# A hybrid decoder layer on one core: compression's layer, the third norm and one 512-column matmul change places, and the end's scaling, joint and stores are divided anew

## The chip, the cores and the metric

The kernel runs on one core of a Trainium2 chip. The metric is the device time of one execution in microseconds; the number given for a kernel is the median of several executions. A separate execution was taken by the hardware profiler; its rows tell when each instruction ran. The engines are TensorE (PE in the profile, with its weight loads as PEld), VectorE (DVE), ScalarE (ACT), GpSimd (POOL) and SyncE (SP, which here only issues transfers). Each engine runs its own instructions in the order of its queue, and the engines wait for one another by semaphores.

## The reference

One decoder layer on 256 tokens of 1024 channels, all in float32, then a final norm:

```python
def reference(x, mem, ...):
    h = rms_norm(x, norm_mix_g)
    x = x + hybrid_mixer(h, ...)              # convolution branch and sparse attention, gated, one projection
    h = rms_norm(x, norm_x_g)
    x = x + cross_attention(h, mem, xq_w, xkv_w, xo_w)
    h = rms_norm(x, norm_ffn_g)
    x = x + swiglu(h, ffn_in_w, ffn_out_w)    # (silu(a) * b) @ w_out
    return rms_norm(x, final_norm_g)

def rms_norm(x, g):
    return x * lax.rsqrt(jnp.mean(x * x, axis=-1, keepdims=True) + EPS) * g

def compress_blocks(blocks, pos, w1, w2):     # keys and values of the attention, by blocks of 32 tokens
    z = jnp.einsum("bnlgd,lde->bnge", blocks + pos, w1)
    return jax.nn.silu(z) @ w2                # "compression's layer" below is this second product
```

## The kernel before

Activations lie with channels on the 128 partitions and tokens along the row. A weight of the projections comes in chunks of 256 columns (`u0`..`u7`, `kc`, `vc`, `q0`.., `ga0`..`ga3`, `gc0`.., `f0`..`f21` and so on), each in two halves of 512 KB that SyncE loads in the order of the list into four rotating buffers.

To keep float32's accuracy on the faster one-pass matmul, each half is split: ScalarE copies it to a rounded high part (line 184, names ending in `h`), and VectorE or GpSimd subtracts that from the original to get the low part (line 186, names ending in `l`). One chunk is then 48 matmuls of 256 columns (line 266): high by high, high by low and low by high, 16 each. `gemm` runs a chunk, `sweep` one half of it, and `rows` is the generator below both. Small products (`c_ps`, `gt_ps`, `rn`, the transposes) are done with plain float32 operands in several passes.

A chunk's result goes to a bank of PSUM, the accumulator memory: `bank()` hands out four in turn, in the stages that matter here.

The order of the work on each engine is made when the program is built: a scheduler goes through the code in the order in which it is written and places the instructions by its own model of their times. Three tools bend it. `in_line()` puts a TensorE instruction behind the last one so marked, `behind(...)` does it for any marks, and `turn(...)` chains the instructions of VectorE and of ScalarE at the very end. On the chip the order is then fixed, engine by engine.

The five places that the change and the prediction touch:

- **u chunks** (lines 494 to 502): eight chunks for the convolution branch. Ahead of `u2` stands a *settle*: one matmul of 512 columns (line 248) whose result is overwritten and not used.
- **Compression** (lines 561 to 600): `hidden()` runs the first product behind `q1`, and `compressed()` the second (`c_ps`), called from within `ga0`, behind a part of its second half. `part` then splits its result by a ScalarE copy and a VectorE subtraction into `kcp` and `vcs`. Between `vw` and `ga0` stands `g_ps`, the heads' gates, which ScalarE copies to `sgn`; `gt_ps` turns them and `sgt` is their exponential. `gt_ps` and the attention's `s0` use one and the same bank. `compressed_scores` (`cs_ps`) needs `kcp`. GpSimd makes `vcm` from `vcs`.
- **Third norm** (lines 1248 to 1266): the feed-forward stage starts on channels that aren't normalised yet. `rooted_all` sums the squares of a token over partitions (`rn`, line 359), ScalarE takes the root (line 362, with a table load ahead of it, since the engine holds one set of functions at a time), and VectorE the reciprocal (line 363). Each chunk's result is scaled by it when VectorE reads it out (`ab`, line 1264), which frees the bank. `f0` and `f1` run ahead of the norm's matmul. A settle stands ahead of `f3`.
- **The f stage's transfers**: SyncE issues the loads of `f` in order, with the eight transfers of the turned residual (line 1132) between `f4`'s first half and its second.
- **The end** (lines 1404 to 1448): the output of the layer is summed for the first 128 tokens (tb = 0) and the last 128 (tb = 1). For each, `total` adds the residual, `gained` multiplies by the final norm's gain, `square` sums squares on ScalarE, `joint` adds a part's sum to the rest, `rooted` takes the root, and `sent` inverts it, scales 672 columns on VectorE and 352 on ScalarE and stores both pieces.

Of the kernel before, what the change touches and what calls it, by code (L numbers as in the profile page):

```python
# [12 lines left out]
ALU = mybir.AluOpType  # L13
# [84 lines left out]
def tile_hybrid_block(  # L98
# [42 lines left out]
    def small(name, shape, dt=F32, tag=None, bufs=1):  # L141
        if len(shape) == 2 and shape[1] < LINE:
            return sb.tile([P, LINE], dt, tag=tag or name, name=name, bufs=bufs)[:, 0:shape[1]]
        return sb.tile(shape, dt, tag=tag or name, name=name, bufs=bufs)
# [79 lines left out]
    def halved(name, i):  # L224
        return split(raw(name, i), [P, 4, 256], f"{name}_{i}")
# [20 lines left out]
    def settle(ps, x):  # L246

        return nc.tensor.matmul(ps.rearrange("p b q -> p (b q)"), lhsT=x[:, 0, 0:P], rhs=x[:, 0:2].rearrange("p k q -> p (k q)"), start=True, stop=True)

    def settled(ps, x):  # L250

        with in_line():
            last[:] = [settle(ps, x)]
# [17 lines left out]
    def sweep(*args, **kw):  # L271
        for _ in rows(*args, **kw):
            pass
# [3 lines left out]
    def gemm(name, x, nat=False, ps=None):  # L277

        ps = bank(f"ps_{name}") if ps is None else ps
        for i in range(2):  # L280
            sweep(ps, ahead_of_x.pop(f"{name}_{i}", None) or halved(name, i), x, i, nat, name in in_order)
        return ps
# [210 lines left out]

    for j in range(NB):
        ps = bank(f"ps_u{j}")
        if j == 2:
            settle(ps, hh)
        gemm(f"u{j}", h, ps=ps)
        sg = small(f"sg{j}", [P, S], tag="sg", bufs=3)
        act = nc.scalar.activation(sg, ps[:, 1], AF.Sigmoid)  # L500
        vec = nc.vector.tensor_tensor(out=vt[j][:, PAD:], in0=ps[:, 0], in1=sg, op=ALU.mult)
        convolve(13 * (j > 0), (0, 1, 1, 1, 1, 0, 1, 1)[j], act, vec)
# [83 lines left out]
    def compressed():  # L586

        c_ps = aux("c_ps", [P, 3, HD], "o", 1)
        kc_ps, vc_ps = c_ps[:, 0].rearrange("p (g n) -> p g n", g=GROUPS), c_ps[:, 1:3]
        with in_line():  # L590
            nc.tensor.matmul(kc_ps, lhsT=ppt[:, PP_W2K:PP_W2K + P], rhs=zz[:, 0, :64].rearrange("p (g n) -> p g n", g=GROUPS),
                             start=True, stop=True)
            for i in range(2):
                mm = nc.tensor.matmul(vc_ps[:, i], lhsT=zz[:, 1, i * P:i * P + P], rhs=ppt[:, PP_W2V:PP_W2V + HD],
                                      start=True, stop=True)
        last[:] = [mm]
        part(kcp[:, :, 0], kcp[:, :, 1], kc_ps)
        part(vcs[:, 0], vcs[:, 1], vc_ps)
# [52 lines left out]
    with in_line():  # L651
        for n, x in enumerate(h):
            for kb in range(NB):
                mm = nc.tensor.matmul(g_ps, lhsT=wgs[:, kb].rearrange("p c n -> p (c n)"), rhs=x[:, kb],
                                      start=n + kb == 0, stop=n * kb == NB - 1)
    last[:] = [mm]
    sgn = small("sgn", [P, S], tag="sg", bufs=3)
    igd = small("igd", [P, HEADS, 2, 2])
    igc = small("igc", [P, 2, HEADS])
# [48 lines left out]
    def gate(j):  # L708

        ps = bank(f"ps_ga{j}")  # L710
        for i in range(2):
            for n, _ in enumerate(rows(ps, halved(f"ga{j}", i), h, i)):
                if j == 1 and i + n == 0:
                    compressed_scores(0)
                if j == 0 and (i, n) == (1, 0):
                    compressed()
        halved_tangent(j, ps)

    gate(0)
# [526 lines left out]
    nc.sync.dma_start(gf[:, 0:2], gfo)  # L1246
    homes.append(gf[:, 2:4])
    ahead_of_norm = []
    for j in range(2):
        ahead_of_norm.append(bank(f"ps_f{j}"))  # L1250
        for i in range(2):
            sweep(ahead_of_norm[j], halved(f"f{j}", i), (fg[:, 0], fg[:, 1]), i, line=j == i == 1)
    with in_line():
        rf = rooted_all([acc2], "3", ("vw", 4))
    for j in range(NF):
        if j < 2:
            ps = ahead_of_norm[j]
        else:
            ps = bank(f"ps_f{j}")
            if j == 3:  # L1260
                settle(ps, fg[:, 0])
            gemm(f"f{j}", (fg[:, 0], fg[:, 1]), ps=ps)
        ab = small(f"ab{j}", [P, 2, S], tag="pr", bufs=4)
        scaled[:] = [nc.vector.tensor_tensor(out=ab, in0=ps, in1=rf.unsqueeze(1).to_broadcast([P, 2, S]), op=ALU.mult)]  # L1264
        sl = small(f"sl{j}", [P, S], tag="sg", bufs=3)
        silu = nc.scalar.activation(sl, ab[:, 0], AF.Silu)  # L1266
        nc.vector.tensor_tensor(out=sl, in0=sl, in1=ab[:, 1], op=ALU.mult)
        marks = part(uh[j // 8][:, j % 8], ul[j // 8][:, j % 8], sl[:])
        if 8 <= j and not (j % 2 and j // 2 in SEVEN):
            with behind(*marks):  # L1270
                next(in_pieces, None)
        if j == 12:
            coming.append(paired(SEVEN[1], homes[:1]))
            coming.append(paired(SEVEN[2], [small(f"t{n}_{SEVEN[2]}", [P, 1, 512], tag="p0", bufs=2) for n in range(2)]))
        if j == 16:
            spare.append(long("spare", 10, (P, 4, 512)))
            homes.append(spare[0][:, 2:4])
            coming.append(paired(SEVEN[3], homes[1:]))
        if j // 2 in SEVEN:
            even_odd.append(sl)  # L1280
            if j % 2:
                factors(j // 2, *even_odd)
                even_odd.clear()
        if j == 2:
            turn_residual()
# [113 lines left out]
    def turn(eng, make, *args):  # L1399

        with behind(*chained.get(eng, ())):
            chained[eng] = make(*args),
# [2 lines left out]
        return nc.vector.tensor_tensor(out=ys[1][tb][:, cs], in0=ps, in1=more[2 * tb + 1][:, cs], op=ALU.add)  # L1405

    def joint(tb, n):
        return nc.vector.scalar_tensor_tensor(out=ss[:, tb, 0:1], in0=ss[:, tb, n:n + 1], scalar=1.0 / D, in1=ss[:, tb, 0:1],
                                              op0=ALU.mult, op1=ALU.add)

    def rooted(tb, n):
        return nc.scalar.activation(rr[:, tb:tb + 1], ss[:, tb, n:n + 1], AF.Sqrt, scale=1.0 / D, bias=ss[:, tb, 0:1])

    def sent(tb, eng):

        x, r, cut, rows = x3[:, tb].rearrange("p c n -> p (c n)"), rr[:, tb:tb + 1], 352, slice(tb * P, tb * P + P)
        turn("v", nc.vector.reciprocal, r, r)
        turn("v", lambda: nc.vector.tensor_scalar(out=x[:, cut:], in0=x[:, cut:], scalar1=r, scalar2=None, op0=ALU.mult))
        turn("a", lambda: nc.scalar.activation(x[:, :cut], x[:, :cut], AF.Copy, scale=r))
        eng.dma_start(out[rows, :cut], x[:, :cut])  # L1420
        nc.sync.dma_start(out[rows, cut:], x[:, cut:])

    ws = {i: half(wfo[i, :, 2:4], f"fo{i}_1") for i in range(early, NF // 2)}
    for i, w in ws.items():
# [11 lines left out]
    turn("a", square, 0, 1, wide, 1)  # L1436
    turn("a", rooted, 0, 1)
    turn("v", total, 1, steps[0], ends[0])
    turn("a", square, 1, 1, steps[0], 1)
    sent(0, nc.sync)  # L1440
    turn("v", gained, 1, 1, steps[0])
    turn("v", total, 1, steps[1], ends[1])
    turn("v", joint, 1, 1)
    turn("v", lambda: nc.vector.tensor_tensor_reduce(out=junk[:, 1, 1, steps[1]], in0=ys[1][1][:, steps[1]], in1=ys[1][1][:, steps[1]],
                                                     scale=1.0, scalar=0.0, op0=ALU.mult, op1=ALU.add, accum_out=ss[:, 1, 2:3]))
    turn("v", gained, 1, 1, steps[1])
    turn("a", rooted, 1, 2)
    sent(1, nc.scalar)


_OUTS = [((S, D), "float32")]
# [120 lines left out]
```

## Time and profile before

| | us |
|---|---|
| median of 3 executions | 527.72 |
| lowest and highest | 526.9 and 527.84 |
| the profiled execution | 526.18 |
| its span, first to last instruction | 524.4 |
| TensorE busy in it | 516.8 |
| mean granted clock of TensorE | 0.996 of full |

The views read are the page's busy shares, the waits (who waited for whom, total, times, longest), the chain of waits in order of time (start, duration, engine, what, line and number of instructions), the timeline of an engine (start, duration, engine, line, operation, output and input, shape and count; in brackets idle time before it and what ended it), and the windows. In the chain and the timeline, neighbours of one kind are merged into one row, so the duration is that of the whole row. The chain counts a matmul from the end of the one before it, the timeline from its own start, so the two differ by a fraction of a microsecond at each row.

### The profile page before, as it was taken

How to read it: one execution, taken by the hardware profiler on the slowest of the kernel's cores; microseconds unless marked ns; L12 is line 12 of the kernel's file. 1: busy time of each engine (PE TensorE's matmuls, PEld its weight loads, DVE VectorE, ACT ScalarE, POOL GpSimd, SP SyncE). 2: the span in 40 equal slices, each digit the busy share in tenths (PEclk: the TensorE clock that was granted, in tenths of full speed). 3: DMA queues.
4: the chain of work that ended last, by engine and by line, in shares of the span. 5: the costliest groups of instructions: out<-in, count | busy, mean ns of one | idle time of the engine just before them, and what ended most of it. 6: DMA issues, size and time to landing. Idle time of an engine off the chain costs nothing.

```text
span 524.4 us, 11134 instructions
## 1 busy us (share of the span) xinstructions
PE 516.8 (99%) x4287; PEld 499.9 (95%) x4287; DVE 436.2 (83%) x883; ACT 345.0 (66%) x605; POOL 160.8 (31%) x114
## 2 busy tenths in 40 slices
PE   9999999999999999999999999999999999999994
PEld 8999999999999999999999999999999999988884
DVE  4866999899979798974968586797998888779985
ACT  5585576788756988879547754756665665558553
POOL 0069999999970300300004100150000000000021
PEclk9999999999999999999999999999999999999998
DMA  8927965665435543348665663879765657755552
GB/s 317 416 94 247 362 204 162 201 206 178 161 116 173 179 163 129 128 136 227 208 203 201 234 163 119 288 223 284 258 228 197 203 179 235 221 134 187 201 125 95
DMA packets 34772, 104.69 MB, mean 200 GB/s; under 512 B 3744, under 2 KB 9376, under 8 KB 34336
## 3 DMA queue, kind: packets, MB, share of 16 engines
q1 hardware_dynamic: 32704, 99.36, 56.2%
q0 software_dynamic: 1296, 3.41, 4.0%
q10 hardware_dynamic: 720, 1.23, 0.6%
q8 instruction: 33, 0.54, 0.4%
q14 instruction: 19, 0.16, 0.1%
HBM read 100.64 MB, written 2.29 MB: 196 GB/s over the span
## 4 chain that ended last, share of the span: by engine, by line
PE 98%; DVE 1%; ACT 0%; issue 0%; DVEq 0%; ACTq 0%
PE ps_f L266 23%; PE ps_u L266 8%; PE fo L1298 6%; PE ps_v L266 4%; PE ps_ga L266 4%; PE ps_pw L266 4%; PE ps_q L266 4%; PE ps_gc L266 4%; PE ps_xo L266 4%; PE ps_xq L266 4%; PE ps_wo L266 4%; PE m L1298 4%; PE ps_k L266 3%; PE s L778 2%; PE pt_a L823 1%; PE o L844 1%
## 5 line engine op out<-in xcount | busy, mean ns | idle before, releaser
L462 DVE SCALAR_TENSOR_TENSOR yp<-vt,ppt,yp 128x256 f32<-128x256 f32 x204 | 81.6, 480 | 0.2
L266 PE MATMUL ps_f<-g,f_1h 128*128 128x256 f32 x352 | 44.4, 276 | 0.0
L266 PE MATMUL ps_f<-g,f_0h 128*128 128x256 f32 x352 | 44.0, 277 | 0.0
L266 PEld LDWEIGHTS ps_f<-g,f_1h 128*128 128x128 f32 x352 | 42.0, 188 | 0.0
L266 PEld LDWEIGHTS ps_f<-g,f_0h 128*128 128x128 f32 x352 | 41.9, 188 | 0.1
L186 DVE TENSOR_TENSOR f_1l<-f,f_1h 128x1024 fp32r<-128x1024 f32 x22 | 27.4, 1248 | 7.4 <-ACT f_1h L184 6.7
L184 ACT ACTIVATE f_1h<-f 128x1024 fp32r<-128x1024 f32 x22 | 23.3, 1059 | 15.0 <-PE ps_f L266 8.3
L184 ACT ACTIVATE f_0h<-f 128x1024 fp32r<-128x1024 f32 x22 | 23.2, 1056 | 12.4 <-issue 6.5
L186 DVE TENSOR_TENSOR f_0l<-f,f_0h 128x1024 fp32r<-128x1024 f32 x22 | 27.2, 1238 | 0.5 <-ACT f_0h L184 0.5
L186 POOL TENSOR_TENSOR u_0l<-u,u_0h 128x1024 fp32r<-128x1024 f32 x7 | 17.4, 2481 | 30.3 <-DVE kt L551 30.3
L1172 POOL DMA_DIRECT2D spare<-in_wfo_dram x1 | 0.9, 866 | 81.7 <-DVE ul L313 81.7
L266 PE MATMUL ps_f<-g,f_0l 128*128 128x256 f32 x176 | 23.7, 276 | 0.0
L266 PE MATMUL ps_f<-g,f_1l 128*128 128x256 f32 x176 | 23.6, 276 | 0.0
L266 PEld LDWEIGHTS ps_f<-g,f_0l 128*128 128x128 f32 x176 | 21.7, 188 | 0.0
L266 PEld LDWEIGHTS ps_f<-g,f_1l 128*128 128x128 f32 x176 | 21.6, 188 | 0.0
L798 ACT ACTIVATE p<-p,mins 128x256 f32<-128x256 f32 x32 | 15.9, 502 | 7.9 <-DVE mins L783 7.9
L1264 DVE TENSOR_TENSOR ab<-ps_f,r 128x512 f32<-128x512 f32 x22 | 14.9, 687 | 4.0 <-PE ps_f L266 4.0
L186 POOL TENSOR_TENSOR u_1l<-u,u_1h 128x1024 fp32r<-128x1024 f32 x7 | 18.0, 2569 | 0.0
L1266 ACT ACTIVATE sl<-ab 128x256 f32<-128x256 f32 x22 | 9.0, 418 | 12.4 <-DVE ab L1264 12.4
L474 POOL TENSOR_TENSOR yt<-yt,vw 128x512 f32<-128x512 f32 x13 | 17.1, 1319 | 0.0
L266 PE MATMUL ps_u<-hh,u_0h 128*128 128x256 f32 x128 | 16.3, 277 | 0.0
L266 PE MATMUL ps_u<-hh,u_1h 128*128 128x256 f32 x128 | 16.0, 276 | 0.0
(624 smaller groups left out, 1620.3 us busy)
## 6 DMA issues: line engine op xcount, KB each, us to landing
f<-in_wst_dram SPq DMA_DIRECT2D x44, 512.0 KB, 3.8
fo<-in_wfo_dram SPq DMA_DIRECT2D x16, 512.0 KB, 4.8
u<-in_wst_dram SPq DMA_DIRECT2D x14, 512.0 KB, 7.8
q<-in_wst_dram SPq DMA_DIRECT2D x8, 512.0 KB, 4.5
ga<-in_wst_dram SPq DMA_DIRECT2D x8, 512.0 KB, 3.7
gc<-in_wst_dram SPq DMA_DIRECT2D x8, 512.0 KB, 4.2
v<-in_wst_dram SPq DMA_DIRECT2D x8, 512.0 KB, 6.1
pw<-in_wst_dram SPq DMA_DIRECT2D x8, 512.0 KB, 4.6
```

The costliest lines, as they stand in the source:

```text
L184: copy = nc.scalar.activation(hi, w, AF.Copy)
L186: splits[name] = copy, eng.tensor_tensor(out=lo, in0=w, in1=f(hi[:]), op=ALU.subtract)
L266: mm = nc.tensor.matmul(ps[:, b], lhsT=lhsT, rhs=rhs, start=row + b + kb == 0, stop=kb == NB - 1 and row == 2 and b == 1)
L462: nc.vector.scalar_tensor_tensor(out=out[:, i] if t == ts[-1] else acc[i], in0=v, scalar=w, in1=acc[i], op0=ALU.mult, op1=ALU.add)
L474: nc.gpsimd.tensor_tensor(out=yt[:, 0:2], in0=yt[:, 0:2], in1=pr, op=ALU.add)
L778: nc.tensor.matmul(s1, lhsT=qh(hd, 1), rhs=t[:, g].rearrange("p b t -> p (b t)"), start=i == 0, stop=i == 1)
L798: exp.append(nc.scalar.activation(p1[k][:, br], p1[k][:, br], AF.Exp, scale=-1.0, bias=mins[:, hd, 1, br:br + 1], accum_out=sums[:, hd, 1, ...
L823: mm = nc.tensor.transpose(ps[:, i], src, ident)
L844: mm = nc.tensor.matmul(o_ps[HD * k:HD * k + HD, i], lhsT=vst[:, 0, br, gs], rhs=ta[k][:, 2 * br:2 * br + 2].rearrange("p t q -> p (t q)") ...
L1264: scaled[:] = [nc.vector.tensor_tensor(out=ab, in0=ps, in1=rf.unsqueeze(1).to_broadcast([P, 2, S]), op=ALU.mult)]
L1266: silu = nc.scalar.activation(sl, ab[:, 0], AF.Silu)
L1298: mm = nc.tensor.matmul(o, lhsT=a[x], rhs=b[w], start=start and n == 0, stop=stop and n == 2)
```

## The change

Five edits, none of which changes what is computed.

1. The settle ahead of `u2` is put ahead of `u1`, and `u0`'s first half is put in line with it.
2. `compressed()` is called right behind `g_ps`, and not within `ga0`.
3. `f2`'s first half runs ahead of the third norm's matmul, as `f0` and `f1` do.
4. `joint`, which adds one column to another with a factor, moves from VectorE to ScalarE, and is called earlier.
5. The first tokens' last scaling is 256 columns on VectorE and 768 on ScalarE, and was 672 and 352. They are stored in two pieces, both from SyncE's queue, the 256 columns first. The last tokens' scaling stays as it was.

```diff
     for j in range(NB):
         ps = bank(f"ps_u{j}")
-        if j == 2:
-            settle(ps, hh)
-        gemm(f"u{j}", h, ps=ps)
+        if j == 1:
+            settled(ps, hh)
+        for i in range(2):
+            sweep(ps, halved(f"u{j}", i), h, i, line=i + j == 0)
...
     last[:] = [mm]
+    compressed()
     sgn = small("sgn", [P, S], tag="sg", bufs=3)
...
                 if j == 1 and i + n == 0:
                     compressed_scores(0)
-                if j == 0 and (i, n) == (1, 0):
-                    compressed()
...
-    for j in range(2):
+    for j in range(3):
         ahead_of_norm.append(bank(f"ps_f{j}"))
-        for i in range(2):
-            sweep(ahead_of_norm[j], halved(f"f{j}", i), (fg[:, 0], fg[:, 1]), i, line=j == i == 1)
+        for i in range(2 - j // 2):
+            sweep(ahead_of_norm[j], halved(f"f{j}", i), (fg[:, 0], fg[:, 1]), i, line=j == 2)
     with in_line():
         rf = rooted_all([acc2], "3", ("vw", 4))
     for j in range(NF):
-        if j < 2:
+        if j < 3:
             ps = ahead_of_norm[j]
+            if j == 2:
+                sweep(ps, halved("f2", 1), (fg[:, 0], fg[:, 1]), 1, line=False)
...
     def joint(tb, n):
-        return nc.vector.scalar_tensor_tensor(out=ss[:, tb, 0:1], in0=ss[:, tb, n:n + 1], scalar=1.0 / D, in1=ss[:, tb, 0:1],
-                                              op0=ALU.mult, op1=ALU.add)
+        return nc.scalar.activation(ss[:, tb, 0:1], ss[:, tb, n:n + 1], AF.Identity, scale=1.0 / D, bias=ss[:, tb, 0:1])
...
-    def sent(tb, eng):
-
-        x, r, cut, rows = x3[:, tb].rearrange("p c n -> p (c n)"), rr[:, tb:tb + 1], 352, slice(tb * P, tb * P + P)
-        turn("v", nc.vector.reciprocal, r, r)
-        turn("v", lambda: nc.vector.tensor_scalar(out=x[:, cut:], in0=x[:, cut:], scalar1=r, scalar2=None, op0=ALU.mult))
-        turn("a", lambda: nc.scalar.activation(x[:, :cut], x[:, :cut], AF.Copy, scale=r))
-        eng.dma_start(out[rows, :cut], x[:, :cut])
-        nc.sync.dma_start(out[rows, cut:], x[:, cut:])
+    def inverted(tb):
+        turn("v", nc.vector.reciprocal, rr[:, tb:tb + 1], rr[:, tb:tb + 1])
+
+    def scaled_by(tb, cs, eng):
+
+        x, r = x3[:, tb].rearrange("p c n -> p (c n)")[:, cs], rr[:, tb:tb + 1]
+        if eng == "v":
+            turn("v", lambda: nc.vector.tensor_scalar(out=x, in0=x, scalar1=r, scalar2=None, op0=ALU.mult))
+        else:
+            turn("a", lambda: nc.scalar.activation(x, x, AF.Copy, scale=r))
+        return out[tb * P:tb * P + P, cs], x
...
     turn("v", total, 1, steps[0], ends[0])
+    inverted(0)
+    nc.sync.dma_start(*scaled_by(0, slice(768, 1024), "v"))
     turn("a", square, 1, 1, steps[0], 1)
-    sent(0, nc.sync)
     turn("v", gained, 1, 1, steps[0])
+    turn("a", joint, 1, 1)
+    nc.sync.dma_start(*scaled_by(0, slice(0, 768), "a"))
     turn("v", total, 1, steps[1], ends[1])
-    turn("v", joint, 1, 1)
...
     turn("a", rooted, 1, 2)
-    sent(1, nc.scalar)
+    inverted(1)
+    nc.sync.dma_start(*scaled_by(1, slice(352, 1024), "v"))
+    nc.scalar.dma_start(*scaled_by(1, slice(0, 352), "a"))
```

What stands in TensorE's queue around `ga0` and `ga1`, before (each row a line of the kernel, operation, output and inputs, shape and count):

```order
L654 MATMUL g_ps_1876<-hh_84,wgs_1873 128x256 x16
L266 MATMUL ps_ga0_1900<-hh_84,ga0_0h_1903 128x256 x16
L266 MATMUL ps_ga0_1900<-hh_84,ga0_0l_1904 128x256 x8
L266 MATMUL ps_ga0_1900<-hh_84,ga0_1h_1933 128x256 x8
L591 MATMUL c_ps_1945<-zz_351,ppt_66 128x64
L594 MATMUL c_ps_1945<-ppt_66,zz_351 128x64 x2
L266 MATMUL ps_ga0_1900<-hh_84,ga0_1h_1933 128x256 x8
L266 MATMUL ps_ga0_1900<-hh_84,ga0_1l_1934 128x256 x8
L266 MATMUL ps_ga1_1977<-hh_84,ga1_0h_1980 128x256 x8
L755 MATMUL gt_ps_2062<-cpt_67,sgn_1893 128x48 x2
L740 MATMUL cs_ps0_1992<-kcp_1172,qt_1176 128x32 x16
```

And now, from the same `g_ps` on, without three rows of `ga1`:

```order
L655 MATMUL g_ps_1876<-hh_84,wgs_1873 128x256 x16
L592 MATMUL c_ps_1893<-zz_351,ppt_66 128x64
L595 MATMUL c_ps_1893<-ppt_66,zz_351 128x64 x2
L266 MATMUL ps_ga0_1908<-hh_84,ga0_0h_1911 128x256 x16
...
L740 MATMUL cs_ps0_1992<-kcp_1172,qt_1176 128x32 x16
...
L266 MATMUL ps_ga1_1977<-hh_84,ga1_1l_2030 128x256 x8
L755 MATMUL gt_ps_2062<-cpt_67,sgn_1901 128x48 x2
L778 MATMUL s1_0_2075<-kdh_1537,qt_1176 128x512
L778 MATMUL s1_0_2075<-kdl_1538,qt_1176 128x512
L778 MATMUL s1_1_2083<-kdh_1537,qt_1176 128x512
L778 MATMUL s1_1_2083<-kdl_1538,qt_1176 128x512
L780 MATMUL s0_0_2073<-kdh_1537,qt_1176 128x256
```

Compression's three products moved 32 matmuls forward, and `gt_ps` moved back to just ahead of the first scores.

In ScalarE's queue at the third norm, before (`f4_1h` is the high part of `f4`'s second half, `r_3` the norm's root, `sl0` the first chunk's silu):

```order
L184 ACTIVATE f3_1h_4975<-f3_1_4973 128x1024
L184 ACTIVATE f4_0h_5020<-f4_0_5018 128x1024
L362 ACT_TABLE_LOAD
L362 ACTIVATE r_3_4843<-rn_3_4841,eps_t_69 128x256
L184 ACTIVATE f4_1h_5050<-f4_1_5048 128x1024
L184 ACTIVATE f5_0h_5088<-f5_0_5086 128x1024
L1266 ACT_TABLE_LOAD
L1266 ACTIVATE sl0_4848<-ab0_4846 128x256
```

And now:

```order
L184 ACTIVATE f3_1h_4975<-f3_1_4973 128x1024
L184 ACTIVATE f4_0h_5020<-f4_0_5018 128x1024
L184 ACTIVATE f4_1h_5050<-f4_1_5048 128x1024
L362 ACT_TABLE_LOAD
L362 ACTIVATE r_3_4874<-rn_3_4872,eps_t_69 128x256
L184 ACTIVATE f5_0h_5088<-f5_0_5086 128x1024
L1268 ACT_TABLE_LOAD
L1268 ACTIVATE sl0_4879<-ab0_4877 128x256
```

The high part of `f4`'s second half has moved ahead of the root and its table load.

## Prediction

> **What bounds the kernel now.** I read the page's busy shares first, then the waits, then the chain in order of time, and the timelines of single engines last. The busy shares put TensorE at 99%, with every other engine behind it:
>
> ```profile
> PE 516.8 (99%) x4287; PEld 499.9 (95%) x4287; DVE 436.2 (83%) x883; ACT 345.0 (66%) x605; POOL 160.8 (31%) x114
> ```
>
> Of waits, TensorE has one row, at the kernel's start:
>
> ```profile
> PE warm L377 <- DVE eps_t L167: 1.1, 1, 1.1
> ```
>
> So TensorE bounds all but the last microseconds. An edit ahead of the end counts only if it changes how long TensorE's own instructions take, or makes it wait. The chain (start, duration, name, instructions) shows that equal instructions do not always take equal time:
>
> ```profile
> 30.15 9.87 PE ps_u L266 x86
> ...
> 131.99 1.88 PE g_ps L654 x16
> 133.87 3.77 PE ps_ga L266 x32
> ...
> 138.26 2.79 PE ps_ga L266 x24
> 141.05 0.38 PE gt_ps L755 x4
> 141.42 1.76 PE cs_ps L740 x16
> ...
> 353.08 0.43 PE rn L359 x2
> 353.51 4.83 PE ps_f L266 x41
> 358.34 0.23 PE ps_f L248
> 358.57 103.36 PE ps_f L266 x912
> ```
>
> A 256-column matmul takes 113.3 ns in the last row (103.36/912), but 117.8 ns in the 32 ahead of compression's layer (3.77/32) and in the 41 behind the third norm (4.83/41). I call the two states quick and slow; they differ by 4.5 ns a matmul. The slow state holds until something resets it: compression's matmuls do (the 24 behind them, with one restart in the sum, average 2.79/24 = 116.3, and that restart explains most of the rest), and the 512-column matmul of L248 does. The windows (busy, instructions, granted clock) show that the clock is the same in both:
>
> ```profile
> 133.87:137.64 3.77, 3.77 (x35) 1.00 0.47 176
> 358.70:369.50 10.80, 10.80 (x97) 1.00 0.99 319
> ```
>
> **The change part by part.** The profiled execution took 526.18 us, of which its span is 524.4 and 1.78 lies around it; it is 1.54 below the median of the runs, 527.72. I make the sum against 526.18 and carry the difference over to the median. A measurement of this kernel can tell about 0.2% from no change, which is 1.06 us.
>
> *The 512-column matmul* moves from u2 to u1 and takes its 0.23 us in either place. The 86 matmuls ahead of its old place average 114.8 ns (9.87/86), one restart included, so they are quick and it resets nothing there: 0. Bounds: −0.17, were the other 38 of u1's 48 matmuls slow in other executions (38 × 4.5 ns), and +0.1 for one more restart.
>
> *Compression's layer* moves from within ga0 to right behind g_ps. The 32 matmuls of ga0 at 117.8 ns then stand behind the reset: 32 × 4.5 ns = −0.14. Its inputs are made long before, so it waits for nothing. Its two ScalarE copies now precede sgn, and gt_ps, which needs sgn, falls behind ga1, ahead of the 512-column s instead of cs_ps. The timeline of TensorE has the price of s behind such a matmul in plain float32, and then of the same s without:
>
> ```profile
> 225.23 0.50 PE L778 MATMUL s<-kdh,qt 128*128 128x512 f32 x1
> ...
> 226.03 0.39 PE L778 MATMUL s<-kdh,qt 128*128 128x512 f32 x1
> ```
>
> That is +0.11, a restart. cs_ps loses its own neighbour, which I put at −0.09, so +0.02 together. The move makes one new wait possible: s0 writes the bank of gt_ps and needs the ScalarE exponential that reads it (L758), which is queued behind sga (L706). ScalarE's rows and the first s on TensorE:
>
> ```profile
> 141.46 0.25 ACT L758 ACTIVATE sgt<-gt_ps 128x96 f32<-128x96 f32 x1 [0.43 <-PE gt_ps L755]
> ...
> 147.66 0.39 PE L778 MATMUL s<-kdh,qt 128*128 128x512 f32 x1
> ...
> 147.97 0.58 ACT L706 ACTIVATE sga<-ps_ga 128x512 f32<-128x512 f32 x1
> ```
>
> Ahead of sga, gt_ps's 0.38 and the 0.14 are gone, so it starts near 147.45 and the exponential ends near 148.3. TensorE runs gt_ps until about 147.5 and then four 512-column matmuls (0.23 each), so s0 stands at 148.5. The cover is some 0.2 us; were it gone, TensorE and all behind it would wait as long. On GpSimd, vcm (4.05 us) passes ahead of ga2's last low part:
>
> ```profile
> 141.04 2.35 POOL L186 TENSOR_TENSOR ga_1l<-ga,ga_1h 128x1024 fp32r<-128x1024 f32 x1
> ...
> 146.98 4.05 POOL L725 TENSOR_TENSOR vcm<-vcs,cpt 128x512 fp32r<-128x512 f32 x4
> ```
>
> That part was done at 143.4 and is done before 149 now; ga2 begins some 3 us behind the first s and uses it 40 matmuls (4.5 us) later, near 155. The sync queue's gc loads that wait for its buffer slip by the same 5 us, within the same cover. Part: −0.14 + 0.02 = −0.12, bounds −0.25 (no restart) and +0.3 (s0 waits).
>
> *The third norm* moves behind f2's first half. Of the 41 slow matmuls 17 then stand ahead of it: 17 × 4.5 ns = −0.08. But on ScalarE, which runs its queue in order, the root now stands behind the split of f4's second half, and that split waits for its load. The rows of the sync queue, ScalarE, VectorE and TensorE:
>
> ```profile
> 352.79 1.05 SPq L221 DMA_DIRECT2D f<-in_wst_dram  x2
> ...
> 353.56 1.28 ACT L362 ACT_TABLE_LOAD   x1
> 354.85 0.48 ACT L362 ACTIVATE r<-rn,eps_t 128x256 f32<-128x256 f32 x1
> 358.80 1.06 ACT L184 ACTIVATE f_1h<-f 128x1024 fp32r<-128x1024 f32 x1 [3.47 <-DMA f<-in_wst_dram]
> ...
> 355.36 1.75 DVE L363 RECIPROCAL r<-r 128x256 f32<-128x256 f32 x1 [0.56 <-ACT r L362]
> 359.89 1.23 DVE L186 TENSOR_TENSOR f_1l<-f,f_1h 128x1024 fp32r<-128x1024 f32 x1 [2.78 <-ACT f_1h L184]
> 361.03 1.88 DVE L1264 TENSOR_TENSOR ab<-ps_f,r 128x512 f32<-128x512 f32 x3
> ...
> 363.85 1.98 PE L266 MATMUL ps_f<-g,f_0h 128*128 128x256 f32 x16
> ```
>
> Before, the root was done at 355.33, and ScalarE's 3.47 us wait for the load delayed nothing else. Now the root waits it out too: split 358.80 to 359.86, table load to 361.14, root to 361.63, reciprocal to 363.41 (VectorE has done f4's low part by then), the first ab (1.88/3) to 364.1. Four banks hold f0 to f3, so f4 starts when that ab has freed f0's. TensorE gets there at 363.85 − 0.12 − 0.08 = 363.65: it waits 0.45, and restarts for 0.11 as above. f5's bank is freed 0.6 later and needed 5.4 later, so this is the only wait; VectorE's rows behind it have that much room as well. The landing decides its size: half a microsecond earlier and nothing is left of it, one later and it is 1.6. Part: −0.08 + 0.56 = +0.48, bounds −0.08 and +1.5.
>
> The Trainium skill ("ScalarE: Activation LUTs", section "What ACT_TABLE_LOAD costs") puts a switch of tables at about 2.66 us, the load and a drain of 1.38 together. By that the root would come 1.38 us later and the sum would be as much higher, 529.3 against the median. The rows speak against it: the root starts 1.29 us behind the load's start, and I give it no chance apart from the late cases below.
>
> *The end.* VectorE and ScalarE in turn, behind TensorE's last matmul; the first row is a scaling of 256 columns elsewhere:
>
> ```profile
> 159.78 0.34 DVE L810 TENSOR_SCALAR p<-p,sums 128x256 f32<-128x256 f32 x1
> ...
> 517.33 0.57 DVE L1418 TENSOR_SCALAR x<-x,rr 128x672 f32<-128x672 f32 x1
> 517.55 0.28 PE L1298 MATMUL end<-fo_1l,uh 128*128 128x256 f32 x1
> 517.60 0.57 ACT L1419 ACTIVATE x<-x,rr 128x352 f32<-128x352 f32 x1
> 518.15 0.42 DVE L1405 TENSOR_TENSOR y<-end,more 128x256 f32<-128x256 f32 x1
> 518.60 0.43 DVE L1444 CUSTOM_DVE_ANT_0 x<-y 128x256 f32<-128x256 f32 x1
> 519.07 0.30 ACT L1412 ACTIVATE rr<-ss 128x1 f32<-128x1 f32 x1 [0.90 <-DVE ss L1444]
> ```
>
> VectorE's first scaling shrinks from 672 to 256 columns, from 0.57 to 0.34. The last sum moves from 518.15 to 517.92, still behind TensorE's end at 517.83. The joint leaves VectorE too, but the custom square began only 0.03 behind the sum's end (518.57), so its going wins 0 to 0.03. The second root could then start at 518.84 instead of 519.07. ScalarE must be free by then: at 517.60 it now does the joint (bounded by the one-column root's 0.30), then 768 columns, which cost 0.87 on the line through 352 columns (0.57) and 1024 (1.06, above). Overlapped as they are, that ends between 518.7 and 518.85: just in time. The sync queue issues three stores instead of two of these and one: 256 columns near 517.7, 768 near 518.85, 672 near 520.0, none behind another. I take −0.20, bounds −0.26 and +0.2.
>
> Sum: 0 − 0.12 + 0.48 − 0.20 = +0.16, so 526.34 for an execution like the profiled one and **527.9** against the median: no change that can be told.
>
> **The rivals.**
>
> *Slower: the wait at f4 leaves TensorE slow.* The f loop has one reset, at f3, ahead of the wait. Should TensorE restart slow, f4 to f21, 18 × 48 = 864 matmuls, cost 4.5 ns more each, 3.9 us: 531.8 against the median. For it speak the 41 behind the norm, and 40 elsewhere at 117.8 ns until transposes came:
>
> ```profile
> 230.92 4.71 PE ps_v L266 x40
> ```
>
> Against it: behind a plain wait ahead of u0 TensorE got quick by itself, 130 ns each with the restart in the first ten, then 113.8:
>
> ```profile
> 27.95 1.30 PE ps_u L266 x10
> 29.25 0.91 PE ps_k L266 x8
> ```
>
> It decides from any wait at f4, however short. Chance 0.17.
>
> *No wait: f4's load lands half a microsecond or more earlier.* The f loads land 3.8 us behind their issue in the median, this one nearer 6, so there is room for it:
>
> ```profile
> f<-in_wst_dram SPq DMA_DIRECT2D x44, 512.0 KB, 3.8
> ```
>
> Then the sum is −0.12 − 0.08 − 0.20 = −0.40: 527.3. Ordinary executions are 1.5 us longer than the profiled one, and should a part of that be slow stretches that the new places reset, the lower bounds come on top, down to 526.9. Chance 0.25, half of it near the bound or, with the runs' own scatter (their lowest is 0.8 under the median), past it.
>
> *ScalarE late at the end.* If joint and 768 columns take 0.4 us longer than I took, the second root starts 0.2 later than before instead of 0.2 earlier: 528.3. No row shows 768 columns on ScalarE. The Trainium skill ("ScalarE: Activation LUTs", section "Rules for kernel authors") gives such multiplies and adds to VectorE, which speaks for this rival. Chance 0.08.
>
> *The moves win nothing:* the states hang on something else than the order, and only the wait and the end are left, 0.22 above the forecast (with the u1 edit at 0): 528.1. The Trainium skill ("TensorE: Matmul & The Clock Gate", section "Step-by-step: what each phase is for") has weight loads run ahead, beside the running matmul, without taking from it; by that rule a 256-column matmul costs the same in every place. The 117.8 and 113.3 ns at one clock speak against it. Chance 0.05.
>
> **How the numbers follow.** The forecast has 0.45, the four rivals 0.55. Faster by over 0.2%: half of the second rival, 0.12. Slower by over 0.2%: the first, 0.17, and 0.05 of the forecast's cases, those with the load a microsecond late: 0.22. Within: 0.66. The range reaches down to 526.6 (the second rival's 526.9 and some scatter) and up to 529.4 (the forecast with the wait at its upper bound, +1.0, and a late end, +0.4); beyond it lies the first rival and little else.
>
> **What would show it.** In the profile after: ga0's 48 matmuls at about 113.5 ns; gt_ps behind ga1 and no wait at s0; the third norm's root near 361 instead of 354.85, and a wait of TensorE of about half a microsecond ahead of f4, with 113.3 ns behind it; the second root at the end about 1.3 us behind TensorE's last start instead of 1.5. Wrong would be: no wait at f4 because the load landed early, 117.8 ns through the f loop, or the second root released by ScalarE's own scaling instead of VectorE's square.

## The result, and the profile after

| | before | after |
|---|---|---|
| median of the compared executions (6 each) | 527.65 us | 531.8 us |
| lowest and highest | 526.71 and 528.33 | 530.95 and 532.58 |
| the profiled execution, its span | 526.18, 524.4 | 531.16, 529.4 |
| TensorE busy in it | 516.8 | 521.5 |
| mean granted clock | 0.996 | 0.996 |

The ratio is 1.0082, with a 95% interval of 1.0070 to 1.0094: the change makes the kernel 4.2 us slower, where no change was forecast. It is the rival with the wait at f4 that came out, at the time that it named (531.8). Of after, the busy shares of the page first:

```profile
PE 521.5 (99%) x4287; PEld 504.1 (95%) x4287; DVE 436.0 (82%) x882; ACT 344.9 (65%) x606; POOL 161.2 (30%) x114
```

TensorE has as many instructions as before and the same mean clock, and is busy 4.7 us longer. Idle time is not the cause; the instructions themselves take longer. The waits of TensorE in after have one new row of only 0.2 us:

```profile
PE warm L377 <- DVE eps_t L167: 1.1, 1, 1.1
PE ps_f L266 <- DVE ab L1266: 0.2, 1, 0.2
```

The chain of after shows what released f4, and what came behind it:

```profile
353.21 5.91 DMA f<-in_wst_dram
...
359.23 1.07 ACT f_1h L184
...
361.60 0.48 ACT r L362
...
362.11 1.76 DVE r L363
...
363.96 0.70 DVE ab L1266
364.67 0.14 issue
364.81 102.00 PE ps_f L266 x864
466.80 3.23 PE fo L1300 x14
```

The steps are those of the forecast: load, split, root, reciprocal, first read-out, f4. But the 864 matmuls of f4 to f21 take 102.00/864 = 118.1 ns each, where before the row of 912 had 113.3. That is 864 x 4.7 ns = 4.1 us by this view, and 3.91 by the starts (f4 to the first fo: 101.83 after, 97.92 before). The windows of the same stretch (its length, then busy time and instructions of PE, PEld, DVE, ACT and POOL, and the granted clock third from the end) have the clock at 1.00 in both kernels; of after:

```profile
364.81:466.60 101.79, 101.79 (x864) 101.79 (x865) 87.46 (x144) 61.62 (x94) 0.86 (x1) 1.00 0.63 203
```

So the new wait is small (0.38 us by the starts, worked out below), and the state in which it leaves TensorE costs ten times as much.

### The profile page after: what moved, and what is told of

The parts are those of the page before. It is cut to its first block, busy times and chain, and to the rows that moved or that the text cites. A ratio compares the mean times of both kernels' runs of the same rounds, so it can differ in the third digit from the quotient of the medians.

```text
span 529.4 us, 11134 instructions
## 1 busy us (share of the span) xinstructions
PE 521.5 (99%) x4287; PEld 504.1 (95%) x4287; DVE 436.0 (82%) x882; ACT 344.9 (65%) x606; POOL 161.2 (30%) x114
## 4 chain that ended last, share of the span: by engine, by line
PE 95%; DMA 2%; DVE 1%; ACT 1%; issue 0%; ACTq 0%; DVEq 0%; SPq 0%
PE ps_f L266 20%; PE ps_u L266 8%; PE fo L1300 6%; PE ps_v L266 4%; PE ps_ga L266 4%; PE ps_pw L266 4%; PE ps_q L266 4%; PE ps_gc L266 4%; PE ps_xo L266 4%; PE ps_xq L266 4%; PE ps_wo L266 4%; PE m L1300 4%; PE ps_k L266 3%; PE s L778 2%; PE ps_k L298 1%; PE pt_a L823 1%
## 5 line engine op out<-in xcount | busy, mean ns | idle before, releaser
L266 PE MATMUL ps_f<-g,f_1h 128*128 128x256 f32 x352 | 45.8, 281 | 0.0
L266 PE MATMUL ps_f<-g,f_0h 128*128 128x256 f32 x352 | 45.2, 280 | 0.2 <-DVE ab L1266 0.2
L266 PEld LDWEIGHTS ps_f<-g,f_0h 128*128 128x128 f32 x352 | 43.0, 189 | 0.4 <-issue 0.4
L266 PEld LDWEIGHTS ps_f<-g,f_1h 128*128 128x128 f32 x352 | 43.2, 189 | 0.1
```

Source lines behind the costliest of these rows:

```text
L266: mm = nc.tensor.matmul(ps[:, b], lhsT=lhsT, rhs=rhs, start=row + b + kb == 0, stop=kb == NB - 1 and row == 2 and b == 1)
```

## The experiments

Theory A, the one that the result suggests: plain float32 products (the expectations call them four-pass products) and waits leave TensorE slow (118 ns for a 256-column matmul instead of 113.3), and it stays so until a 512-column matmul resets it. Against it stood:

- B: VectorE or ScalarE, now at other work beside the f loop, disturb TensorE.
- C: the place of the norm's product itself decides, which now stands ahead of 24 and not of 41 of the matmuls up to the settle.
- D: the other edits take part.
- E, later: the 512-column matmul does nothing, the state comes and goes.
- F, later: only a wait for a bank does it.

In each run below the kernel before was timed on the same chip; its medians were 527.21 to 527.43.

**The reset behind the wait as well as ahead of it.** After, with the settle at f3 and at f4:

```diff
-            if j == 3:
+            if j in (3, 4):
                 settle(ps, fg[:, 0])
```

> The changed kernel with one 512-column matmul more, ahead of f4, behind the wait there. Theory A (a state: the wait leaves TensorE slow, and a 512-column matmul resets it): the wait of about 0.4 us stays, f4 to f21 run at 113.3 ns instead of 117.9, 864 x 4.6 ns = 3.97 us less and 0.23 for the new matmul: 3.7 below the changed kernel, 528.0 against before's 527.65. Theory B (the f loop is slow because VectorE and ScalarE run later in it and disturb each matmul): still 117.9 ns, and 0.23 above the changed kernel: 532.0.

Measured: ratio 1.0062 (1.0036 to 1.0089), which is a mean over two groups: four executions at 528.05 to 528.34, six at 531.41 to 532.60. The profiled one is of the first group. Its chain:

```profile
360.06 5.45 PE ps_f L266 x48
365.50 0.32 PE ps_f L248
365.82 97.93 PE ps_f L266 x864
```

The settle, which here is the waiting instruction itself, took 0.32 instead of 0.23 us, so it hardly waited in this execution; 97.93/864 = 113.3 ns follows. That speaks against B: the engines beside do what they do in after. It shows no reset behind a wait, since there was hardly a wait. And A as worded would have all ten executions quick. A is incomplete: perhaps a 512-column matmul resets only if it does not itself wait.

**The root ahead of f4's second split.** After, with one mark that puts the split behind the root on ScalarE, as it stood before; TensorE's order is that of after:

```diff
         rf = rooted_all([acc2], "3", ("vw", 4))
+    first["f4_1"] = first["3"][:1]
```

> The changed kernel with f4's second split put behind the third norm's root on ScalarE; TensorE's order is the same. Theory A: the root is done near 357.5, the first ab near 362, no wait at f4, the f loop at 113.3 ns: 4.3 below the changed kernel, 527.4. Theory C (it is the place of the norm's own matmul, the four-pass product within f2, that leaves TensorE slow): the wait is gone but f4 to f21 stay at 117.9 ns: 531.4.

Measured: 527.29, ratio 0.9998 (0.9986 to 1.0009). TensorE has only the start's wait, and the chain reads

```profile
356.12 0.43 PE rn L359 x2
356.55 2.83 PE ps_f L266 x24
359.38 0.23 PE ps_f L248
359.61 103.37 PE ps_f L266 x912
```

113.3 ns throughout, with the norm's product where after has it. C is refuted, and the whole loss is tied to the order of two instructions on ScalarE: the split that waits for its load, and the root behind it.

**The norm's edit alone, and all but it.** Before with only the third edit, and after with the third edit undone:

```diff
-    for j in range(2):
+    for j in range(3):
         ahead_of_norm.append(bank(f"ps_f{j}"))
-        for i in range(2):
+        for i in range(2 - j // 2):
...
-        if j < 2:
+        if j < 3:
             ps = ahead_of_norm[j]
+            if j == 2:
+                sweep(ps, halved("f2", 1), (fg[:, 0], fg[:, 1]), 1, line=False)
```

> The kernel before with the third norm's edit alone. Theory A and C: the whole loss comes with it, -0.08 + 0.45 + 3.9 = +4.3 us, 531.9. Theory D (the other edits have a part in it, for example by where they leave the queues): clearly less than +4.3, say +2 or less.

> The changed kernel with the third norm's edit undone: the 512-column matmul at u1, compression's layer and the end. Theory A and C: no wait at f4, f loop at 113.3 ns; -0.13 for compression's layer, 0 for u1, 0 to -0.2 for the end: 527.4, which the time can't tell from before; the profile shows the parts. Theory D: some of the +4.2 stays, 529 or more.

Measured: alone 531.58, ratio 1.0060 (1.0035 to 1.0086), spread from 526.99 to 532.41; without it 527.38, ratio 1.0001 (0.9990 to 1.0011), with 113.3 ns in the loop. So D is refuted: the other edits have no part in it. In the profiled execution of the edit alone the load landed later (its chain has 6.34 us for it), the wait was longer, and the loop as slow as in after:

```profile
PE ps_f L266 <- DVE ab L1266: 0.6, 1, 0.6
```

Two executions at 527 and two between fall out of this; whether the wait or the 118 ns behind it were missing in them, no trace shows.

**No settle at all.** Before, without the settle at f3, so that TensorE waits nowhere in the stage and only the norm's product stands ahead:

```diff
-            if j == 3:
-                settle(ps, fg[:, 0])
```

> The kernel before, without the 512-column matmul ahead of f3; TensorE waits nowhere in the f stage. Theory A (a state that the norm's four-pass product or a wait sets, and that lasts until a 512-column matmul): the 41 slow matmuls behind the norm go on to f21, 912 x 4.6 ns = +4.2 us, less 0.23 for the matmul left out: 531.4 against 527.4, and about 118 ns in the trace. Theory E (the slow matmuls come from the wait at f4 or pass by themselves; the 512-column matmul does nothing): 527.2, 113.3 ns soon behind the norm.

Measured: 530.86, all four executions within 0.3 us, ratio 1.0069 (1.0052 to 1.0086).

```profile
353.96 0.43 PE rn L359 x2
354.39 112.24 PE ps_f L266 x953
466.63 5.60 PE fo L1296 x24
```

112.24/953 = 117.8 ns without any wait. The state lasts for the 112 us of the loop; E's version, by which it passes, is refuted, and so is the wait as the only cause.

**The settle further behind.** After with a second settle at f5, one chunk behind the wait, and in another kernel at f12:

```diff
-            if j == 3:
+            if j in (3, 5):      # the other kernel: (3, 12)
                 settle(ps, fg[:, 0])
```

> The kernel after, with one more 512-column matmul ahead of f5, one chunk behind the wait. Theory A with its addition (only a 512-column matmul that does not itself wait is sure to reset): 48 slow matmuls (0.2 us) and 0.23 for the added one: 528.2 in all executions, in one group and not in the two (528.2 and 532.0) that the one ahead of f4 gave. Theory E: two groups again, or 531.8.

> The kernel after, with one more 512-column matmul ahead of f12, where nothing waits. Theory A: f4 to f11 slow behind the wait (384 x 4.6 ns = 1.8 us), f12 to f21 quick: 527.9 + 1.8 + 0.2 = 529.9 in executions with the wait, and the step from 118 to 113.3 ns stands at f12 in the trace. Theory E (state left to chance at the restart, the 512-column matmul does nothing): 531.8 and 118 ns through f21, or 528 where the restart happened to be quick.

Measured at f5: 527.48, 526.37 to 529.02, and so none of the ten near 532; ratio 1.0008 (0.9994 to 1.0022). The profiled execution had a long wait, 1.1 us by the waits, since the load took 6.43, and shows the step where the settle stands:

```profile
366.12 5.90 PE ps_f L266 x48
372.01 0.23 PE ps_f L248
372.24 92.49 PE ps_f L266 x816
```

The 48 matmuls of f4 run at 117 to 119 ns behind a first of 194, and the 816 from f5 on at 113.3. This is the cleanest sight of the reset: a settle that does not itself wait, behind the wait.

At f12: 529.0, 526.80 to 530.29, ratio 1.0032 (1.0015 to 1.0049); the forecast was 529.9 with the wait, and none comes near after's 531.8. The profiled execution is one that got quick by itself:

```profile
365.79 43.79 PE ps_f L266 x384
409.58 0.23 PE ps_f L248
409.81 54.41 PE ps_f L266 x480
```

TensorE stood idle for 0.28 us ahead of f4 (from the starts), restarted with 194, 116, 118, 122 and 119 ns, and then had 113 and 114: 43.79/384 = 114.0. In after the idle time was 0.37, and nothing followed the restart but 117 to 119. So the step at f12 is seen only in the times, and A needs an addition: a short stop may pass by itself.

**A settle that itself waits for long.** After with the settle at f3 and f4, and the norm's reciprocal taken three times:

```diff
-        first[name] = root, nc.vector.reciprocal(r, r)
+        first[name] = root, [nc.vector.reciprocal(r, r) for _ in range(3 if name == "3" else 1)][-1]
```

> The kernel after with the 512-column matmul ahead of f4 as well, and the reciprocal of the third norm done three times (the result stays the same), so that this 512-column matmul itself waits 2 x 1.75 = 3.5 us longer in every execution. Theory A with its addition (where the 512-column matmul itself waits for long, it does not reset): slow in all executions, 527.9 + 3.5 + 0.2 + 4.0 = 535.6. Theory A without it: quick, 531.6. Theory E: two groups, 531.6 and 535.6.

Measured: 539.79 in the profiled execution and 534.68 to 535.15 in the four others. The waits and then the windows of the profiled one:

```profile
PE ps_f L248 <- DVE ab L1266: 5.9, 1, 5.9
```

```profile
371.35:374.00 2.65, 2.65 (x11) 2.55 (x12) 2.65 (x4) 1.14 (x3) 0.00 (x0) 0.50 0.61 221
374.00:376.00 2.00, 2.00 (x14) 2.00 (x13) 1.14 (x4) 0.38 (x1) 0.00 (x0) 0.63 0.41 104
400.00:475.00 75.00, 75.00 (x639) 75.00 (x638) 61.06 (x97) 43.29 (x65) 0.87 (x1) 1.00 0.60 195
```

Here the wait grew past the 3.9 us intended, the clock was at half for some 4 us behind it, and then the loop is slow at full clock to its end: 75.00/639 = 117.4 ns. So a settle that is itself the waiting instruction can leave TensorE slow. But it need not: 527.3 with 6.1 of idle time, 2.0 for 17 matmuls and the settle at half clock, and 0.2 for the settle more make 535.6 for a quick loop, and the four other executions lie at 535.1, with the same mean clock (0.991 to 0.992, in the profiled one 0.992). By this sum they were quick, if they waited as long; no trace of them shows it. The addition in its strict form (slow in all) has fallen. What is left is that such a settle isn't sure to reset, as the first experiment's two groups had it.

**A wait for weights instead of a bank.** The kernel with the root first, with f10's first split held back behind f9. The first try held back only its low part:

```diff
         if j == 2:
             turn_residual()
+        if j == 9:
+            first["f10_0"] = scaled[0],
```

> The kernel after with the root ahead of f4's second split (so no wait at f4), and the split of f10's first half held back behind the first product of f9's result: TensorE then waits ahead of f10 for weights and not for a bank, by f9's read-out (0.6) and the split (1.06), some 1.8 us. Theory A (any wait of that length leaves TensorE slow until a 512-column matmul): 576 matmuls x 4.6 ns = 2.65 us besides, 527.3 + 1.8 + 2.65 = 531.7, and 118 ns from f10 to f21. Theory F (only a wait for a bank does, one for weights passes as the restart at u0 did): 529.1, and 113.3 ns.

Measured: 526.60, ratio 0.9989 (0.9979 to 0.9999), and no wait: ScalarE's copy isn't held by a mark on VectorE, so only the low part moved, and f11's first 16 matmuls went ahead of it. It says nothing on F. The second try uses a mark on ScalarE, f9's silu:

```diff
+        if j == 9:
+            first["f10_0"] = silu,
```

> The kernel after with the root ahead of f4's second split, and the whole split of f10's first half held back behind f9's silu on ScalarE (the earlier try held back only its low part, and TensorE did not wait). TensorE now waits ahead of f10 for weights: f9's read-out 0.7, silu 0.4 and the copy 1.06, 2.2 us or a little more. Theory A (any such wait leaves TensorE slow until a 512-column matmul): 527.3 + 2.2 + 576 x 4.6 ns = 532.2, 118 ns from f10 to f21. Theory F (only a wait for a bank does): 529.5, 113.3 ns. Other waits may follow at f11 and f12 while the splits catch up; they would come on top in both.

Measured: 531.89, 530.61 to 532.22, ratio 1.0095 (1.0079 to 1.0111). The waits, and then the windows of the profiled execution:

```profile
PE ps_f L266 <- ACT f_0h L184: 2.2, 1, 2.2
```

```profile
390.00:396.00 6.00, 6.00 (x55) 6.00 (x54) 2.93 (x6) 0.83 (x2) 0.00 (x0) 1.00 0.01 3
396.90:399.30 2.40, 0.19 (x2) 0.00 (x0) 1.56 (x4) 1.38 (x3) 0.00 (x0) 1.00 0.00 0
399.33:400.30 0.97, 0.97 (x8) 0.97 (x9) 0.97 (x2) 0.97 (x2) 0.00 (x0) 1.00 0.00 0
400.30:404.00 3.70, 3.70 (x21) 3.70 (x20) 3.70 (x5) 2.65 (x4) 0.00 (x0) 0.54 0.58 182
404.00:410.00 6.00, 6.00 (x55) 6.00 (x54) 3.79 (x6) 3.06 (x3) 0.00 (x0) 1.00 0.94 292
```

Right behind the wait the matmuls take 117 and 118 ns, as behind the wait for a bank: F is refuted as far as the restart goes. But the 118 ns did not last. After 1.2 us the clock fell to half, and when it came back TensorE was quick, 113.3 ns to f21, without any 512-column matmul. The time of the profiled execution, 530.61, comes from the wait and the half clock and is no support for A. The three others took 531.77 to 532.22. Half the clock for the 3.4 us that 0.54 over 3.7 us amounts to takes 0.003 off the mean over the span, and the one of 532.22 had a mean of 0.999, so it had no such stretch; the wait and 118 ns up to f21, as A has it, would give its time. No trace of it shows which it was.

**The end without the middle store.** The kernel with the root first, without the store of the first tokens' 768 columns:

```diff
-    nc.sync.dma_start(*scaled_by(0, slice(0, 768), "a"))
+    scaled_by(0, slice(0, 768), "a")
```

> The same kernel without the held-back split, and without the store of the first tokens' 768 columns (so a part of the output isn't written; nothing else is left out). With the new end the second root starts 1.30 us behind TensorE's last start instead of 1.5, but the span ends 6.9 behind it as before (6.85). Theory G (the middle store's data occupy the transfer engines when the last tokens' stores arrive): the end falls to 6.65. Theory H (the two last stores just take longer, or the end doesn't hang on the root): 6.9 again. The f stage is as in the kernel with the root first.

Measured in the one execution: the span ends 6.31 us behind TensorE's last start. In six profiles with after's end and all three stores (after, the kernels with a settle more at f4, f5 and f12, the one with the root first and the one without the norm's edit) it is 6.89 to 6.93, and in before, and before without the settle, 6.86 and 6.83. So the end falls as G has it, by 0.6 us instead of 0.25. But G's mechanism isn't shown by it. The last data land 4.86 us behind TensorE's last start here and 5.06 in after, but 4.77 in two kernels with all three stores (the two tries on weights, which end at 6.63 and 6.65). Most of the 0.6 lies behind the last data: 1.45 us to the end of the span instead of 1.83. Why, the trace doesn't show.

The end also moves for another reason. In the profiles of the norm's edit alone and of the last kernel below, VectorE's product with the gain ahead of the second root took 1.79 and 1.54 us instead of 1.04; the root came as much later, and the spans end at 7.59 and 7.11. With the long wait it is 6.83.

**The best version once more.** The first try on weights was, by chance, the fastest kernel so far; it was measured again unchanged:

> The kernel of the earlier try once more, unchanged (root ahead of f4's second split; f10's low part behind f9's read-out, so that f11's first 16 matmuls run ahead of f10's low ones), to tell whether its 0.9989 was more than scatter. By the sum of the traces it should win the 0.12 of compression's layer, the 0.08 of the norm and 0.2 to 0.25 at the end, 0.4 us: 527.0, a ratio of 0.9992. If it was scatter: 527.4, a ratio of 1.000.

Measured: 526.40, 525.81 to 527.10, ratio 0.9983 (0.9974 to 0.9992). It beats before by 0.1 to 0.3% and after by about 1%. The 0.4 us that the expectation adds up lie just inside the interval, but a half of them, the end's, shows only in the profile of the first run of this kernel (6.63 us behind TensorE's last start, and 6.86 in before) and not in this one's (7.11); whether the reordering at f10 brings the rest isn't shown, since its f loop takes 103.36 us for 912 matmuls like that of the kernel with the root first.

## Why the prediction was wrong

The step that failed is a choice, not a term that was overlooked. The forecast let TensorE restart at f4 "for 0.11" and go on at 113.3 ns; the rival had it stay slow for 864 matmuls, with 3.9 us, and got 0.17. The runs showed 118.1 ns for all 864, 3.91 us. The rival should have been the forecast. Two things misled me.

- **The row against the rival was no wait.** I called the restart ahead of u0 "a plain wait" that TensorE recovered from. Its rows in the timeline of before are

```profile
26.88 1.07 PE L266 MATMUL ps_k<-meml,k_1h 128*128 128x256 f32 x8
27.83 1.42 PE L266 MATMUL ps_u<-hh,u_0h 128*128 128x256 f32 x10
```

  From start to start that is 0.95 us for eight matmuls of 0.113, so TensorE stood idle for 0.05 us. At f4 it was 0.37. So u0 was no precedent for a stop of that length. By the executions traced here, stops up to 0.28 us passed and those of 0.37, 0.8, 1.2 and 2.4 us left it slow; where between lies the limit, and whether there is one, one execution each can't tell.
- **The place behind the only reset.** The prediction said that the f loop has one reset, ahead of the wait, and that the state would then hold through 18 chunks. Both were right. Against a term of 3.9 us that hangs on how one restart falls, 0.17 was a price for knowing more than the profile showed.

The other terms, by the starts of TensorE's instructions in the two profiled executions (before, after), from which the start-up has to be taken off: u0's first matmul is at 27.83 and at 28.57, 0.74 later, ahead of anything that the change touches.

- **The settle at u1: 0.** The first of kc is at 75.09 and 75.83, still 0.74. Right for these two executions. In four of the eleven traces with the settle at u1 it did end a slow stretch, so the bound of −0.17 stood for a case that occurs.
- **Compression's layer: −0.12.** The third chunk of the gates is 0.61 late (150.75 and 151.37), so −0.13. Right, and for the reasons given; in the chain of after,

```profile
134.61 0.17 PE c_ps L592 x2
134.78 0.45 PE c_ps L595 x4
135.23 6.42 PE ps_ga L266 x56
141.65 1.69 PE cs_ps L740 x16
```

  6.42 us for 56 is 114.6 ns each, where before had 3.77 + 2.79 = 6.56; gt_ps stands behind ga1 at 147.98, and TensorE doesn't wait at s0.
- **The norm: −0.08 + 0.45 + 0.11.** Ahead of f4 the settle at f3 came 0.58 late instead of 0.66: −0.08, right. The wait with its restart measured 0.38 + 0.08 instead of 0.45 + 0.11. The rows of ScalarE, in the timeline of after, are those that were forecast:

```profile
359.23 1.06 ACT L184 ACTIVATE f_1h<-f 128x1024 fp32r<-128x1024 f32 x1 [5.25 <-DMA f<-in_wst_dram]
360.31 1.28 ACT L362 ACT_TABLE_LOAD   x1
361.60 0.47 ACT L362 ACTIVATE r<-rn,eps_t 128x256 f32<-128x256 f32 x1
```

  The root is at 361.60 for a forecast near 361, and again 1.29 us behind the start of its table load. By the drain that the Trainium skill ("ScalarE: Activation LUTs", section "What ACT_TABLE_LOAD costs") adds to the load it would be 2.66; the rows of after agree with those of before, not with it.
- **The end: −0.20.** The second root starts 1.30 us behind TensorE's last start instead of 1.52, as forecast. But the chain of after has ScalarE's 768 columns ahead of it, and not VectorE's square:

```profile
522.86 0.93 ACT x L1424
523.78 0.01 issue
523.79 0.30 ACT rr L1413
```

  They took 0.92 for a worked-out 0.87, and cost the root some 0.06: the mechanism of the third rival, at a tenth of its price. The 0.2 of the forecast was won at the stores' issue: the last ones left 2.50 instead of 2.71 us behind TensorE's last start. Yet the span ended 6.90 behind it instead of 6.86. The prediction counted the stores' issues, "none behind another", and not what else the transfer engines carry. The view of the transfers in after's last 7 us (522 to 529.4) has, beside the stores, a transfer of 8 KB of instructions:

```profile
q14 instruction: 1, 0.01, 0.3%
```

  By its packet it runs from 3.36 to 3.67 us behind TensorE's last start, among the data of the last stores, and these land 2.56 us behind their issue. In before it comes at 7.46, behind the end of the span, and the data land 2.28 behind their issue. The other traces agree: 2.56 to 2.59 in the six that have it near 3.4, and 2.27 to 2.28 in the six that have it behind the span's end, three of these with the new end and all its three stores. In the other two (the long wait, and the kernel without the middle store) it comes at the end and at the start of these data, and they take 2.42 and 2.37. So this transfer, and not the middle store's data, goes with the 0.28 us. That is a comparison and not a test: no run moves it alone. Net +0.04 instead of −0.20.

The change's own terms are then 0 − 0.13 − 0.08 + 0.38 + 3.91 + 0.04, and 0.07 for first fo matmuls that run at 233 instead of 229 ns behind the slow loop: +4.2 us, and the medians differ by 4.15.

## What to carry to other kernels

Where one state of an engine lasts, price a new wait by how much work stands behind it without a reset, and not by its own length alone: 0.38 us here brought 3.9. Ask for each instruction that is moved ahead of another in a queue whether it waits for a transfer; the root, ready at once, was put behind a split whose load had 5 us to go. And if a precedent decides between two cases, compare its size before its kind: the restart at u0 was a stop of 0.05 us.

## What the runs showed of the hardware

**Two durations at one clock.** One-pass matmuls of 256 columns ran at 113.3 or at 118 ns at one granted clock, in the same place and order of the kernel, and kept to it for up to 953 in a row. Where plain float32 products or stops precede, the outcome can differ from one execution to the next. An example is the second run of ps_k at the kernel's start, where the order is the same: 6.36 us for 56 in before, and 6.59 in before without the settle. In the chain of before, and then of before without the settle:

```profile
11.64 6.36 PE ps_k L266 x56
```

```profile
12.15 6.59 PE ps_k L266 x56
```

What the two states are, the traces don't show: the weight loads start 2 to 5 ns behind a matmul's start in the slow loop, and 3 to 4 in the quick one.

**What ends the slow one.** A single 512-column matmul that stood among 256-column ones and did not itself wait ended the 118 ns each time that a trace shows one behind it. A return from half clock did so once (behind the wait for weights) and once did not (behind the long wait). But this is no rule for any 512-column matmul, as A's wording has it. Behind the loop without a settle, the first 24 matmuls of fo, with 512 columns each, took 5.60 us (the row at 466.63 above), 233 ns each; in before they take 229:

```profile
461.93 5.49 PE fo L1298 x24
```

And the last 24 matmuls of the kernel, with 256 columns, run at 118 ns in every trace, with no stop and no plain float32 product just ahead of them, right behind 512-column ones.

**The clock behind a stop.** A stop of 2.4 us was enough for the granted clock to fall to 0.54 over the 3.7 us from 400.3, some 1.2 us after TensorE had gone back to work. The Trainium skill ("TensorE: Matmul & The Clock Gate", section "Why this matters for your kernels") asks for no gaps over about 3 us between bursts; by this trace a shorter one can already cost a stretch at half clock. It need not, since another execution of the same kernel had a mean clock of 0.999.

**The start-up.** Executions of one kernel differ by some 2 us (the kernel with the root first: 526.00 to 528.32). In the profiles of these kernels, whose TensorE order is the same up to there, u0 is reached between 27.83 and 29.34 us, so 1.5 of it lies in the start-up. There the first matmuls of ps_k in line 298 take up to 427 ns each: none in before, three in after and five in the kernel with the settle at f4; nearly all the others take 215 to 217.
